# Cross-attention queries with features on partitions, and their rms in the exponential's scale

## The chip, the core and the metric

The kernel runs on one core of a Trainium2 chip. The time is device time in microseconds of one execution; the figure to compare is the median of several runs. Engines are named as in the profile: PE is TensorE (matrix products and transposes; PEld its weight loads), DVE is VectorE, ACT is ScalarE, POOL is GpSimd, SP is SyncE, which issues most DMAs.

## What is computed

One layer of a streaming encoder, on 1024 tokens of width 1024 in float32: a mixer (forgetting attention and gated linear attention side by side) with an output projection, cross-attention on 256 memory tokens, and an MLP, each added to the residual `h`. The part that matters here:

```python
def memory_cross_attention(hn, memn, wq, wkv, q_norm_g, k_norm_g, wo):
    B, S, _ = hn.shape                       # 1, 1024
    M = memn.shape[1]                        # 256
    q = rms_norm((hn @ wq).reshape(B, S, XATTN_HEADS, XATTN_HEAD_DIM), q_norm_g)   # 4 heads of 256
    k, v = jnp.split(memn @ wkv, 2, axis=-1)
    k = rms_norm(k.reshape(B, M, XATTN_HEADS, XATTN_HEAD_DIM), k_norm_g)
    v = v.reshape(B, M, XATTN_HEADS, XATTN_HEAD_DIM)
    s = jnp.einsum('bshd,bmhd->bhsm', q, k).astype(jnp.float32) / math.sqrt(XATTN_HEAD_DIM)
    p = jax.nn.softmax(s, axis=-1)
    o = jnp.einsum('bhsm,bmhd->bshd', p.astype(v.dtype), v).reshape(B, S, D_MODEL)
    return o @ wo

h = h + memory_cross_attention(rms_norm(h, norm_xattn_g), rms_norm(mem, norm_mem_g), ...)
```

`rms_norm` divides by the root of the mean square over the last axis, plus an epsilon.

## The kernel before

**Products.** Every float32 operand is split into a high part and a remainder (`sh`/`sl`, `wh`/`wl`, `qh`/`ql`, `th`/`tl`, `oh`/`ol`): ACT writes the high part, DVE the remainder. A product is then three matrix products, high x high, high x remainder, remainder x high (`gemm`, lines L110 to L112). `evac_split` (L117, L118) does such a split out of PSUM.

**Layout.** `self.h` holds the residual with features on partitions: `h[:, k, t]`, eight blocks `k` of 128 features by 1024 tokens. The gain of the norm ahead of the queries is in the weights (`wsplit` with `C_XAT`, L99/L100); the norm's own factor per token goes into the rms of the heads as an epsilon scaled by the token's mean square (`hev`).

**Order of the stages.** `project_out` (L838) makes `h`, in two halves of 512 tokens; for each of eight feature blocks it loads a partial result (`hr`, L851), adds it (L856), squares the block (L169) and adds the square on POOL to `acc` (L170). Four transposes of `acc` per half (`token_squares`, L177) and small operations (L179, L180, L860, L861) then make the tokens' mean squares `hv` and `hev`. Next come `xattn` (L958), `project_o_first` (L879), `project_o_rest` (L887) and the MLP. The instructions are written in this order; the framework's scheduler then reorders each engine's queue by its own estimate of a timeline, places the pools, and sets semaphores, so neighbouring stages overlap, and early MLP weights (`raw` of `in_mlp_w`, split into `g` by L1075/L1076) are loaded and split during cross-attention where room is free.

**Cross-attention.** Two groups `n` of two heads, four units `u` of 256 tokens each, eight units in all. `queries(n, u)` takes 128 tokens at a time: `split_tile` (L819/L820) splits `h` into a 128x1024 pair, 24 products of 512 columns put tokens on partitions (`mm`), ACT squares them (L144), DVE sums per head (L146), POOL makes the rms (L129/L130), DVE scales (`qn`, L995), PE transposes four 128x128 blocks (L998), and `evac_split` writes `qh`, `ql`. `attend(n, u)` comes one unit later: scores of 256 columns per head (`s`), the maximum (L1014), exponentials (L1020), reciprocal (L1021), normalising on POOL (L1024), transposes (L1027), the split `th`/`tl`, the values `pv` in products of 256 columns, and the split `o`, which SP writes to memory (`od`, L1038). `load_o` (L868/L869) reads `od` back for the output projection, whose products carry `mm<-oh,wh`; the first four blocks of that are in `project_o_first`.

Of the kernel before, what the change touches and what calls it, by code (L numbers as in the profile page):

```python
# [51 lines left out]
class Layer:  # L52
# [757 lines left out]

    def split_tile(self, sp, srcs, kt=KT):

        nc = self.nc
        sh = self.T(sp, [P, kt, P], F32R, "sh")
        sl = self.T(sp, [P, kt, P], F32R, "sl")
        k = 0
        for src in srcs:
            w = src.shape[1]
            nc.scalar.activation(sh[:, k:k + w, :], src, AF.Copy)  # L819
            nc.vector.tensor_tensor(sl[:, k:k + w, :], src, f(sh[:, k:k + w, :]), ALU.subtract)  # L820
            k += w
        return [sh[:, k, :] for k in range(kt)], [sl[:, k, :] for k in range(kt)]

# [54 lines left out]

    def project_o_first(self):  # L879

        self.ost, self.O = ExitStack(), {}
        self.load_o(self.open(self.ost, "op0", side="right"), 1)
        self.Wo = self.wsplit(self.wo[:, 0:512], None)
        for i in range(4):
            self.o_block(self.Wo, 0, 1, i, self.T(self.mmp, [P, 512], F32, "mm"))
# [72 lines left out]
    def xattn(self):  # L958
        nc = self.nc
        with ExitStack() as st:  # L960
            kvp = [None, self.open(st, "kv41")]
            qp = self.open(st, "q4", 3)
            qnp = self.open(st, "qn4", 2)
            pp = self.open(st, "p4", 3)
            ptp = self.open(st, "pt4", 2)
            mmp, trp = self.mmp, self.trp
            kst = ExitStack()
            kvp[0] = self.open(kst, "kv40")
            sst = ExitStack()
            sp = self.open(sst, "sp", 2, side="right")  # L970
# [4 lines left out]
            Ws, KV = {}, {}  # L975

            def weights(n):
                Ws[n] = self.wsplit(self.wq[:, n * 512:(n + 1) * 512], C_XAT)
                kT = self.T(kvp[n], [P, 2, 4, M], F32R, "kT")
                nc.sync.dma_start(f(kT), self.kTd[:, :, 4 * n:4 * n + 4, :])  # L980
                vm = self.T(kvp[n], [P, 2, 2, 512], F32R, "vm")
                nc.sync.dma_start(f(vm), self.vmd[:, :, :, n * 512:(n + 1) * 512])
                KV[n] = kT, vm

            def queries(n, u):
                qh = self.T(qp, [P, 2, 4, P], F32R, "qh")
                ql = self.T(qp, [P, 2, 4, P], F32R, "ql")
                for i in range(2):
                    t = 2 * u + i
                    A = self.split_tile(sp, (self.h[:, :, t * P:(t + 1) * P],))  # L990
                    ps = self.T(mmp, [P, 512], F32, "mm")
                    self.gemm(ps, *A, *Ws[n])
                    qn = self.T(qnp, [P, 512], F32, "qn")
                    r = self.head_rstd(ps, qn, 2, self.hev[:, t:t + 1])
                    nc.vector.tensor_tensor(v2(qn), v2(ps), self.bcast(r, 256), ALU.mult)  # L995
                    tp = self.T(trp, [P, 512], F32, "tr")
                    for j in range(4):
                        nc.tensor.transpose(tp[:, j * P:(j + 1) * P], qn[:, j * P:(j + 1) * P], self.ident)  # L998
                    self.evac_split(qh[:, i], ql[:, i], v4(tp))
                return qh, ql  # L1000

            def attend(n, u, q):
                qh, ql = q
                kT, vm = KV[n]
                th = self.T(ptp, [P, 2, 4, P], F32R, "th")
                tl = self.T(ptp, [P, 2, 4, P], F32R, "tl")
                for i in range(2):
                    ps = self.T(sps, [P, 512], F32, "s")
                    for h in range(2):
                        ks = (2 * h, 2 * h + 1)  # L1010
                        self.gemm(ps[:, h * M:(h + 1) * M], [qh[:, i, k, :] for k in ks], [ql[:, i, k, :] for k in ks],
                                  [kT[:, 0, k, :] for k in ks], [kT[:, 1, k, :] for k in ks])
                    nm = self.T(self.smallp, [P, 2], F32, "nm2")
                    nc.vector.tensor_reduce(nm, v2(ps), AX.X, ALU.max, negate=True)  # L1014
                    p = self.T(pp, [P, 512], F32, "p")
                    rs = self.T(self.smallp, [P, 2], F32, "rs2")
                    rr = self.T(self.smallp, [P, 2], F32, "rr2")
                    for h in range(2):
                        c = slice(h * M, (h + 1) * M)
                        nc.scalar.activation(p[:, c], ps[:, c], AF.Exp, bias=nm[:, h:h + 1], accum_out=rs[:, h:h + 1])  # L1020
                    nc.vector.reciprocal(rr, rs)  # L1021
                    for h in range(2):
                        c = slice(h * M, (h + 1) * M)
                        nc.gpsimd.tensor_scalar(p[:, c], p[:, c], rr[:, h:h + 1], 1.0, ALU.mult, ALU.mult)  # L1024
                    tp = self.T(trp, [P, 512], F32, "tr")
                    for j in range(4):
                        nc.tensor.transpose(tp[:, j * P:(j + 1) * P], p[:, j * P:(j + 1) * P], self.ident)  # L1027
                    self.evac_split(th[:, i], tl[:, i], v4(tp))
                for h in range(2):
                    pv = self.T(pvp, [P, 2, 2, P], F32, "pv")  # L1030
                    for d in range(2):
                        c = slice((2 * h + d) * P, (2 * h + d + 1) * P)
                        self.gemm(pv[:, d], [vm[:, 0, m, c] for m in range(2)], [vm[:, 1, m, c] for m in range(2)],
                                  [th[:, :, 2 * h + m, :] for m in range(2)], [tl[:, :, 2 * h + m, :] for m in range(2)])
                    o = self.T(pp, [P, 2, 2, 256], F32R, "o")
                    self.evac_split(o[:, 0], o[:, 1], pv.rearrange("p d t s -> p d (t s)"))
                    for i in range(2):
                        nc.sync.dma_start(self.od[:, i, u // 2, 4 * n + 2 * h:4 * n + 2 * h + 2,  # L1038
                                                  u % 2 * 256:u % 2 * 256 + 256], f(o[:, i]))

            units = [(0, u) for u in range(4)] + [(1, u) for u in (2, 3, 0, 1)]
            q = []
            for i, (n, u) in enumerate(units):
                if i % 4 == 0:
                    weights(n)
                q.append(queries(n, u))
                if i >= 1:
                    attend(*units[i - 1], q[i - 1])
                if i == 4:
                    kst.close()  # L1050
            sst.close()
            attend(*units[-1], q[-1])
            self.project_o_first()

# [286 lines left out]
```

## Time and profile before

| | |
|---|---|
| median of 3 runs | 1450.64 us (1450.14 to 1451.19) |
| the profiled execution | 1454.34 us |
| its span, first to last instruction | 1452.6 us |
| mean granted clock of PE | 0.996 |
| PE busy | 1427.7 us, 98% of the span |
| DVE, ACT, POOL busy | 65%, 47%, 27% |
| cross-attention, about | 592 to 755 us of the span |

How the rows below are read. In a timeline row stand the start in us, the length in us, engine, line, operation, out<-in by the program's names, shapes, how many were put together (x2), and in brackets the idle time before it on its engine and what ended that. Matrix products overlap, so the time from start to start counts, not the length. A windows row has the stretch, its length, the busy time and count of PE, PEld, DVE, ACT, POOL, then the granted clock of PE (1.00 is full), the share of the DMA engines and GB/s. A waits row has the waiting engine, tile and line, what ended the wait, and then total us, number, and longest. A groups row has line, engine, operation, tiles, shapes and count, then busy us and the mean of one in ns, then idle time ahead of them. Rows of two numbers and an engine are pieces of the chain of work that ended last.

### The profile page before, as it was taken

The page shows a single profiled execution, that of the slowest core. Times are in us where ns is not written, and L with a number is a line of the kernel's source. Part 1 is how long each engine was busy: PE and PEld are TensorE (multiplying, and loading weights), DVE is VectorE, ACT ScalarE, POOL GpSimd, SP SyncE. Part 2 cuts the span into 40 slices and gives each one's busy share as a digit, 9 for nine tenths or more (in the row PEclk, how much of TensorE's full clock was granted, in tenths as well). Part 3 has the DMA queues.
Part 4 walks back from the last instruction along what each step waited for, and adds up shares of the span by engine and source line. Part 5 has one row for each costly group of instructions (what it writes and reads, how often), then busy time and mean ns, then how long its engine had stood idle before and what let it go on. Part 6 is the DMA issues. An engine that isn't in the chain of part 4 may idle for free.

```text
span 1452.6 us, 19224 instructions
## 1 busy us (share of the span) xinstructions
PE 1427.7 (98%) x7068; PEld 1190.0 (82%) x7068; DVE 948.6 (65%) x1354; ACT 679.9 (47%) x1095; POOL 397.1 (27%) x404
## 2 busy tenths in 40 slices
PE   9999999998999999999999999999999999999998
PEld 7788788887888887888888878887888888888887
DVE  5366732428798776666644895636556968788796
ACT  4444341327678565455542364445546735335230
POOL 3235513312242223521212300000000542333454
PEclk9999999999999999999999999999999999999999
DMA  8435520268677642412474124444445835336353
GB/s 273 128 73 131 138 70 1 73 176 252 203 211 234 188 140 87 132 59 88 150 266 170 51 80 153 174 174 189 174 174 209 322 121 188 131 122 225 119 198 119
DMA packets 121166, 223.94 MB, mean 154 GB/s; under 512 B 8912, under 2 KB 54512, under 8 KB 118512
## 3 DMA queue, kind: packets, MB, share of 16 engines
q1 hardware_dynamic: 119776, 218.25, 46.5%
q10 hardware_dynamic: 1296, 4.46, 1.0%
q8 instruction: 56, 0.92, 0.3%
q14 instruction: 38, 0.31, 0.1%
HBM read 150.59 MB, written 72.09 MB: 153 GB/s over the span
## 4 chain that ended last, share of the span: by engine, by line
PE 71%; issue 16%; DMA 6%; DVE 3%; ACT 2%; POOL 1%; ACTq 0%; SPq 0%; DVEq 0%; POOLq 0%
PE mm L110 13%; PE mm L112 13%; PE mm L111 13%; PE my L111 5%; PE my L112 5%; PE my L110 5%; PE tr L111 2%; PE tr L112 2%; PE tr L110 2%; PE tr L696 2%; PE pv L703 1%; DMA xt<-in_x_dram 1%; DMA raw<-in_w_in_dram 1%; PE pv L704 1%; PE s L656 1%
## 5 line engine op out<-in xcount | busy, mean ns | idle before, releaser
L111 PE MATMUL my<-x,g 128*128 128x512 f32 x464 | 180.6, 389 | 1.3 <-DVE x L1076 1.3
L110 PE MATMUL my<-x,g 128*128 128x512 f32 x464 | 180.6, 390 | 0.4 <-ACT h L1281 0.4
L112 PE MATMUL my<-x,g 128*128 128x512 f32 x464 | 180.5, 389 | 0.0
L111 PE MATMUL mm<-wl,xh 128*128 128x512 f32 x320 | 126.5, 396 | 0.9 <-DVE wl L100 0.8
L110 PE MATMUL mm<-wh,xh 128*128 128x512 f32 x320 | 126.0, 397 | 1.0 <-DVE sq L307 1.0
L112 PE MATMUL mm<-wh,xl 128*128 128x512 f32 x320 | 125.9, 394 | 0.0
L1075 ACT ACTIVATE g<-s 128x1024 fp32r<-128x1024 f32 (+1 forms) x72 | 68.7, 962 | 105.0 <-PE my L112 39.1
L1076 DVE TENSOR_TENSOR g<-raw,g 128x512 fp32r<-128x512 f32 (+3 forms) x72 | 69.2, 964 | 67.6 <-ACT g L1075 67.4
L111 PEld LDWEIGHTS my<-x,g 128*128 128x128 f32 x464 | 87.1, 188 | 19.9 <-DVE x L1076 1.7
L1101 POOL TENSOR_TENSOR s<-raw 128x384 f32<-128x384 f32 (+1 forms) x20 | 25.8, 1291 | 282.7 <-DVE h L1196 213.8
L110 PEld LDWEIGHTS my<-x,g 128*128 128x128 f32 x464 | 87.1, 188 | 18.8 <-ACT h L1281 0.8
L1075 ACT ACTIVATE g<-raw 128x512 fp32r<-128x512 f32 (+3 forms) x72 | 55.5, 773 | 100.3 <-DMA raw<-in_mlp_w_dram 40.1
L112 PEld LDWEIGHTS my<-x,g 128*128 128x128 f32 x464 | 87.1, 188 | 17.9
L667 POOL TENSOR_SCALAR p<-p,rrec 128x128 f32<-128x128 f32 (+3 forms) x64 | 57.9, 907 | 159.2 <-DVE rrec L666 151.9
L1076 DVE TENSOR_TENSOR g<-s,g 128x1024 fp32r<-128x1024 f32 (+1 forms) x72 | 88.2, 1228 | 7.6 <-ACT g L1075 7.5
L1243 DVE TENSOR_TENSOR x<-x 128x1024 fp32r<-128x1024 f32 (+1 forms) x64 | 76.8, 1220 | 17.3 <-ACT x L1242 17.1
L110 PE MATMUL mm<-x,g 128*128 128x512 f32 x220 | 85.8, 390 | 0.0
L112 PE MATMUL mm<-x,g 128*128 128x512 f32 x220 | 85.7, 389 | 0.0
L111 PE MATMUL mm<-x,g 128*128 128x512 f32 x220 | 85.6, 389 | 0.0
L110 PE MATMUL tr<-x,g 128*128 128x512 f32 x212 | 82.5, 389 | 0.0
L111 PE MATMUL tr<-x,g 128*128 128x512 f32 x212 | 82.5, 389 | 0.0
L112 PE MATMUL tr<-x,g 128*128 128x512 f32 x212 | 82.5, 389 | 0.0
(318 smaller groups left out, 3739.2 us busy)
## 6 DMA issues: line engine op xcount, KB each, us to landing
ud<-h SPq DMA_DIRECT2D x32, 768.0 KB, 3.8
x<-ud SPq DMA_DIRECT2D x48, 512.0 KB, 5.3
raw<-in_mlp_w_dram SPq DMA_DIRECT2D x20, 1024.0 KB, 7.4
raw<-in_mlp_w_dram SPq DMA_DIRECT2D x16, 768.0 KB, 6.0
raw<-in_w_in_dram SPq DMA_DIRECT2D x23, 512.0 KB, 5.0
raw<-in_xattn_wkv_dram SPq DMA_DIRECT2D x16, 512.0 KB, 7.4
od<-o SPq DMA_DIRECT2D x32, 256.0 KB, 4.0
ud<-h SPq DMA_DIRECT2D x32, 256.0 KB, 2.8
```

Source lines behind the costliest of these rows:

```text
L110: mm(ps, lh[k], rh[k], start=start and k == 0, stop=False, **kw)
L111: mm(ps, lh[k], rl[k], start=False, stop=False, **kw)
L112: mm(ps, ll[k], rh[k], start=False, stop=stop and k == n - 1, **kw)
L656: nc.tensor.matmul(ps[:, c], qa[:, ts], ka[:, c], start=True, stop=False)
L667: nc.gpsimd.tensor_scalar(p[:, 0:n], p[:, 0:n], rr, 1.0, ALU.mult, ALU.mult)
L696: nc.tensor.transpose(o, pp[i][:, kb * P:(kb + 1) * P], self.ident)
L703: nc.tensor.matmul(pv, va[:, kb, :], th[:, js], start=kb == 0, stop=False)
L704: nc.tensor.matmul(pv, va[:, kb, :], tl[:, js], start=False, stop=kb == nb - 1)
L1075: self.nc.scalar.activation(hi, src, AF.Copy)
L1076: self.nc.vector.tensor_tensor(lo, src, f(hi), ALU.subtract)
L1101: eng.tensor_tensor(s[:, 0], raw[:, 3], raw[:, 2], ALU.add)
L1243: nc.vector.tensor_tensor(lo, f(lo), f(hi), ALU.subtract)
```

## The change

The queries are made with features on partitions, for 512 tokens at a time. The weights are the stationary side, the split `h` the moving side. So nothing is transposed to get `q`. Its rms is not applied to `q`: the squares of a head's two feature blocks are added on POOL, transposed (four 128x128 blocks for two blocks of features), summed on DVE, and POOL makes `rq`, which is the `scale=` of the exponential and multiplies the maximum. There are four units of 512 tokens, in the order (n, half) = (0, 0), (0, 1), (1, 1), (1, 0). The values become products of 512 columns, and `od` is written by 16 DMAs of 512 KB instead of 32 of 256 KB. The pool of split `h` holds 12 pairs of 512 columns (48 KB a partition, 16 KB before), keys and values have one buffer, which is loaded again at the third unit, and the last unit's scores and values stand between the loads and blocks of the output projection. `split_tile` and `project_o_first` are gone. In the changed kernel lines behind 810 move: the h addition is L842, the loads of `oh`/`ol` L854/L855, squares L981, their addition L985, their transposes L988, exponentials L1018, POOL's normalising L1022, transposes of p L1025, `od` L1039, the MLP's splits L1096/L1097.

```diff
+            def query(u, W, A, j):
+                ps = self.T(mmp, [P, 512], F32, "mm")
+                c = slice(j * P, (j + 1) * P)
+                self.gemm(ps, *([w[:, c] for w in w_] for w_ in W), *zip(*A))
+                q = self.T(qp, [P, 2, 512], F32R, "q")
+                self.evac_split(q[:, 0], q[:, 1], ps)
+                Q.setdefault(u, []).append(q)
+                sq = self.T(sqp, [P, 512], F32, "sq")
+                nc.scalar.activation(sq, ps, AF.Square)
+                if j % 2 == 0:
+                    self.sq0 = sq
+                    return
+                nc.gpsimd.tensor_tensor(sq, sq, self.sq0, ALU.add)
+                tp = self.T(trp, [P, 512], F32, "tr")
+                for t in range(4):
+                    nc.tensor.transpose(tp[:, t * P:(t + 1) * P], sq[:, t * P:(t + 1) * P], self.ident)
+                ss = self.T(self.smallp, [P, 4], F32, "ss4")
+                nc.vector.tensor_reduce(ss, v4(tp), AX.X, ALU.add)
+                nc.gpsimd.tensor_scalar(ss, ss, 1.0 / 256, None, ALU.mult)
+                half = units[u][1]
+                nc.gpsimd.tensor_tensor(ss, ss, self.hev[:, 4 * half:4 * half + 4], ALU.add)
+                if j == 1:
+                    R[u] = self.T(self.smallp, [P, 2, 4], F32, "rq")
+                nc.gpsimd.tensor_tensor(R[u][:, j // 2, :], ss, self.mhalf[:, 0:4], ALU.pow)
...
+            def scores(u, t):
...
+                r = R[u][:, :, t]
+                nc.vector.tensor_reduce(nm, v2(ps), AX.X, ALU.max, negate=True)
+                nc.vector.tensor_tensor(nm, nm, r, ALU.mult)
...
-                        nc.scalar.activation(p[:, c], ps[:, c], AF.Exp, bias=nm[:, h:h + 1], accum_out=rs[:, h:h + 1])
+                    nc.scalar.activation(p[:, c], ps[:, c], AF.Exp, bias=nm[:, h:h + 1], scale=r[:, h:h + 1], accum_out=rs[:, h:h + 1])
...
+            def values(u):
...
+                for j in range(4):
+                    pv = self.T(pvp, [P, 512], F32, "pv")
+                    c, ms = slice(j * P, (j + 1) * P), (2 * (j // 2), 2 * (j // 2) + 1)
+                    self.gemm(pv, *([vm[:, i, m, c] for m in range(2)] for i in range(2)),
+                              [th[:, m] for m in ms], [tl[:, m] for m in ms])
...
+                    nc.sync.dma_start(self.od[:, :, half, 4 * n + j, :], f(o))
...
-            sp = self.open(sst, "sp", 2, side="right")
+            sp = self.open(sst, "sp", 12, side="right")
...
+            for u, (n, half) in enumerate(units):
+                if u % 2 == 0:
+                    W = self.wsplit(self.wq[:, n * 512:(n + 1) * 512], C_XAT)
+                if u == 0:
+                    memory(0)
+                    A = split(half, range(KT))
+                keep = A
+                for j in range(4):
+                    if j == 3 and u in (0, 2):
+                        A = split(units[u + 1][1], range(4))
+                    query(u, W, keep, j)
+                    if u and j < 2:
+                        scores(u - 1, 2 * j)
+                        scores(u - 1, 2 * j + 1)
+                    elif u and j == 2:
+                        values(u - 1)
+                        if u == 2:
+                            memory(1)
+                if u in (0, 2):
+                    A = A + split(units[u + 1][1], range(4, KT))
             sst.close()
-            attend(*units[-1], q[-1])
-            self.project_o_first()
+            self.ost, self.O = ExitStack(), {}
+            self.load_o(self.open(self.ost, "op0", side="right"), 1)
+            self.Wo = self.wsplit(self.wo[:, 0:512], None)
+            for t in range(4):
+                scores(3, t)
+            for i in range(4):
+                if i == 2:
+                    values(3)
+                self.o_block(self.Wo, 0, 1, i, self.T(self.mmp, [P, 512], F32, "mm"))
```

Three places where the order of an engine changes. Numbers behind names tell buffers apart; brackets name the semaphores that an instruction waits for, by the engine or DMA queue that raises them.

First, ACT at the end of project_out, where the first splits of `h` for the queries stand. Before, two 128x1024 splits (`sh_6226`, `sh_6271`) stand among the squares of the second half, without a wait:

```order
L169 ACTIVATE sqT_5970<-h_5805 128x512 [waits DVE_49,Pool_49]
L169 ACTIVATE sqT_5983<-h_5805 128x512 [waits DVE_49,Pool_49]
L819 ACTIVATE sh_6226<-h_5805 128x1024
L819 ACTIVATE sh_6271<-h_5805 128x1024
L166 ACTIVATE acc_1376_5813<-h_5805 128x512 [waits DVE_49]
L169 ACTIVATE sqT_6045<-h_5805 128x512 [waits DVE_49,Pool_49]
```

After, the first split of 512 columns stands behind the last square:

```order
L99 ACTIVATE wh_6743<-raw_6741,cols_74 128x512 [waits DMAHW2_49,PE_49]
L169 ACTIVATE sqT_6122<-h_5805 128x512 [waits DVE_49,Pool_49]
L169 ACTIVATE sqT_6135<-h_5805 128x512 [waits DVE_49,Pool_49]
L117 ACTIVATE sh_6221<-h_5805 128x512 [waits DMAHW4_49,DMAHW5_49,DMAHW3_49,DMAHW6_49,DMAHW0_49,DMAHW7_49,PE_49,Pool_49]
L117 ACTIVATE sh_6225<-h_5805 128x512
L117 ACTIVATE sh_6229<-h_5805 128x512
```

What moved: the first split now waits for loads of `hr`, for PE's last transpose of `acc` (`tr_6138`) and for POOL's last addition (of `sqT_6135`); the larger pool lies on the room of project_out's `acc`, `sqT` and `hr`.

Second, PE there. Before, the transposes of `acc` stand between query products, 39 products behind the last of project_out:

```order
L110 MATMUL mm_6275<-wh_6202,sh_6271 128x512
L111 MATMUL mm_6275<-wl_6203,sh_6271 128x512
L112 MATMUL mm_6275<-wh_6202,sl_6272 128x512
L177 MATMUL tr_6138<-ident_75,acc_1376_5813 128x128 [waits Pool_49]
L177 MATMUL tr_6138<-ident_75,acc_1376_5813 128x128 x3
L110 MATMUL mm_6275<-wh_6206,sh_6271 128x512
L111 MATMUL mm_6275<-wl_6207,sh_6271 128x512
```

After, they stand between project_out's last product (`mm_6127`) and the first query product (`mm_6253`):

```order
L111 MATMUL mm_6127<-sl_6009,wh_5840 128x512
L112 MATMUL mm_6127<-sh_6008,wl_5841 128x512
L177 MATMUL tr_6138<-ident_75,acc_1376_5813 128x128 [waits Pool_49]
L177 MATMUL tr_6138<-ident_75,acc_1376_5813 128x128 x3
L110 MATMUL mm_6253<-sh_6221,wh_6179 128x512 [waits DMAHW3_49,DMAHW4_49,DMAHW2_49,DMAHW5_49,DMAHW1_49,DMAHW6_49,DMAHW0_49,DMAHW7_49,DVE_49,Activation_49]
L110 MATMUL mm_6283<-sh_6221,wh_6179 128x512
L111 MATMUL mm_6253<-sl_6222,wh_6179 128x512 [waits DVE_49]
```

What moved: the transposes that wait for POOL are now ahead of all query products.

Third, ACT behind the last query product. Before, the last unit's exponentials (`p`) stand among evacuations alone:

```order
L1020 ACTIVATE p_7709,rs_1777_7710<-s_7694,nm_1775_7707 128x256 [waits DVE_49,Pool_49]
L117 ACTIVATE th_7593<-tr_7648 128x512 [waits PE_49]
L117 ACTIVATE th_7692<-tr_7717 128x512 [waits PE_49,Activation_49]
L1020 ACTIVATE p_7739,rs_1783_7740<-s_7724,nm_1781_7737 128x256 [waits DVE_49,Pool_49]
L117 ACTIVATE o_7668<-pv_7655 128x512 [waits DMAHW7_49,DMAHW1_49,PE_49]
```

After, two splits of MLP weights (`g`) stand ahead of the third of four tiles' exponentials (`p_7577`):

```order
L1018 ACTIVATE p_7546,rs_1753_7547<-s_7530,nm_1751_7543,rq_7264 128x256 [waits DVE_49]
L1096 ACTIVATE g_1846_8203<-raw_1845_8201 128x512 [waits DMAHW3_49]
L1096 ACTIVATE g_1848_8208<-raw_1847_8206 128x512 [waits DMAHW4_49]
L117 ACTIVATE th_7497<-tr_7523 128x4x128 [waits PE_49,Activation_49]
L1018 ACTIVATE p_7577,rs_1759_7578<-s_7561,nm_1757_7574,rq_7264 128x256 [waits DVE_49]
L117 ACTIVATE th_7497<-tr_7554 128x4x128 [waits PE_49]
L117 ACTIVATE o_7398<-pv_7391 128x512 [waits DMAHW6_49,Activation_49]
```

What moved: exponentials of the last tiles are queued behind loads of MLP weights, which SP issues behind the first loads of `oh` and `ol`.

More of the change, by code (lines that the diff above doesn't have):

```diff
@@ L808, in out_part @@
                 yield
[L811 to L822, printed above, removed]
     def split_half(self, sp, src, half, bufs, ks):
@@ L1002, in attend @@
[L1002 to L1028, printed above, removed]
-                for h in range(2):
[L1030 to L1050, printed above, removed]
-            sst.close()
-            attend(*units[-1], q[-1])
-            self.project_o_first()
+            def split(half, ks):
+                out = []
+                for k in ks:
+                    sh = self.T(sp, [P, 512], F32R, "sh")
+                    sl = self.T(sp, [P, 512], F32R, "sl")
+                    self.evac_split(sh, sl, self.h[:, k, half * 512:(half + 1) * 512])
+                    out.append((sh, sl))
+                return out
@@ new lines, in scores @@
+            def scores(u, t):
+                kT = KV[units[u][0]][0]
+                ts = slice(t * P, (t + 1) * P)
+                if t == 0:
+                    TH[u] = [self.T(ptp, [P, 4, 512], F32R, n) for n in ("th", "tl")]
+                ps = self.T(sps, [P, 512], F32, "s")
+                for h in range(2):
+                    ks = (2 * h, 2 * h + 1)
+                    self.gemm(ps[:, h * M:(h + 1) * M], *([Q[u][k][:, i, ts] for k in ks] for i in range(2)),
+                              *([kT[:, i, k, :] for k in ks] for i in range(2)))
+                r = R[u][:, :, t]
+                nm = self.T(self.smallp, [P, 2], F32, "nm2")
+                nc.vector.tensor_reduce(nm, v2(ps), AX.X, ALU.max, negate=True)
+                nc.vector.tensor_tensor(nm, nm, r, ALU.mult)
+                p = self.T(pp, [P, 512], F32, "p")
+                rs = self.T(self.smallp, [P, 2], F32, "rs2")
+                rr = self.T(self.smallp, [P, 2], F32, "rr2")
+                for h in range(2):
+                    c = slice(h * M, (h + 1) * M)
+                    nc.scalar.activation(p[:, c], ps[:, c], AF.Exp, bias=nm[:, h:h + 1], scale=r[:, h:h + 1], accum_out=rs[:, h:h + 1])
+                nc.vector.reciprocal(rr, rs)
+                for h in range(2):
+                    c = slice(h * M, (h + 1) * M)
+                    nc.gpsimd.tensor_scalar(p[:, c], p[:, c], rr[:, h:h + 1], 1.0, ALU.mult, ALU.mult)
+                tp = self.T(trp, [P, 512], F32, "tr")
+                for j in range(4):
+                    nc.tensor.transpose(tp[:, j * P:(j + 1) * P], p[:, j * P:(j + 1) * P], self.ident)
+                self.evac_split(*(v[:, :, ts] for v in TH[u]), v4(tp))
@@ new lines, in xattn @@
+            units = [(0, 0), (0, 1), (1, 1), (1, 0)]
+            A = []
+            for u, (n, half) in enumerate(units):
[5 more added lines that the diff above has]
+                keep = A
+                for j in range(4):
+                    if j == 3 and u in (0, 2):
[10 more added lines that the diff above has]
+                    A = A + split(units[u + 1][1], range(4, KT))
```

46 lines of the change are left out of this document (13 added, 33 removed).

## The prediction

> **What bounds the kernel now.** I read the page's busy shares first, then a window over the whole cross-attention stage, then the waits of PE in that stage.
>
> ```profile
> span 1452.6 us, 19224 instructions
> PE 1427.7 (98%) x7068; PEld 1190.0 (82%) x7068; DVE 948.6 (65%) x1354; ACT 679.9 (47%) x1095; POOL 397.1 (27%) x404
> 592.00:754.00 162.00, 160.74 (x955) 141.39 (x954) 97.56 (x156) 79.18 (x165) 40.31 (x72) 1.00 0.41 135
> PE mm L110 <- DMA oh<-od: 0.8, 1, 0.8
> PE mm L111 <- DMA ol<-od: 0.4, 2, 0.2
> ```
>
> PE works through 160.74 of 162 us at full clock, and its three waits (1.27 us) are all for loads of the attention output at the end. So only PE work removed is a gain, and each new PE wait is a loss. The profiled execution took 1454.34 us, span 1452.6; the median is 1450.64. I sum differences and add them to both.
>
> **PE work removed.** Rows of PE at the start of the stage, one row pair of the values, the group of query transposes, and two pieces of the chain of work:
>
> ```profile
> 591.94 0.39 PE L112 MATMUL mm<-sh,wl 128*128 128x512 f32 x1
> 592.16 0.39 PE L110 MATMUL mm<-wh,sh 128*128 128x512 f32 x1
> 592.39 0.39 PE L111 MATMUL mm<-wl,sh 128*128 128x512 f32 x1
> 742.72 0.28 PE L110 MATMUL pv<-th,vm 128*128 128x256 f32 x1
> 742.84 0.28 PE L111 MATMUL pv<-tl,vm 128*128 128x256 f32 x1
> L998 PE MATMUL tr<-ident,qn 128*128 128x128 f32 x64 | 10.1, 272 | 0.0
> 601.17 0.44 PE tr L177 x4
> 611.17 0.44 PE tr L998 x4
> ```
>
> Starts of neighbours give the pitch: 0.227 us for 512 columns, 0.12 for 256. The 384 query products keep 512 columns, and the 192 score products 256: nothing. The values become 96 products of 512 instead of 192 of 256: 96 x 0.227 = 21.8 against 192 x 0.12 = 23.0, so -1.25. The 64 transposes of `qn` (16 groups of four, 0.44 each on the chain) become 32 of summed squares: 8 x 0.44 = -3.5. Sum -4.75, certain within half a microsecond.
>
> The Trainium skill, page "TensorE: Matmul & The Clock Gate", section "Back-to-back issue gap", gives about 131 ns for a sustained product of 512 columns; the values' 96 products would then be an estimated 12.6 us, a gain of 10.4 instead of 1.25. This trace shows 227 ns for such products, and the sum goes by that row.
>
> ACT and DVE lose scaling and `qn` splits and gain products with r; both have over 60 us idle in the stage. Their sums cost nothing while PE has queued matmuls. The new chain square, POOL addition, transpose, reduce, POOL power ends in `scale=` of an exponential one unit later, with a whole unit's query products (96 x 0.227 = 21.8 us) as cover: 0. The keys and values reloaded at unit 2 into a single buffer have the same cover: 0, at worst the 0.83 that one late load costs PE below.
>
> **The start.** Before, ACT splits the first two token tiles while project_out still runs, so the query product at 592.16 follows the last product of project_out directly; the transposes of the accumulated squares (L177) come 9 us later, between query products. After, `sh_6221` waits for these very transposes and for POOL's last addition, and PE has nothing ahead of its consumer.
>
> ```profile
> 578.46 1.99 ACT L819 ACTIVATE sh<-h 128x1024 fp32r<-128x1024 f32 x2
> 579.60 3.71 DVE L820 TENSOR_TENSOR sl<-h,sh 128x1024 fp32r<-128x1024 f32 x2 [0.63 <-ACT sh L819]
> 586.60 3.35 SPq L80 DMA_DIRECT2D raw<-in_xattn_wq_dram  x2
> 590.17 0.94 SPq L851 DMA_DIRECT2D hr<-hpd  x2
> 594.90 1.34 DVE L856 TENSOR_TENSOR h<-mm,hr 128x512 f32<-128x512 f32 x2 [2.10 <-DMA hr<-hpd]
> 595.68 1.28 ACT L169 ACTIVATE sqT<-h 128x512 f32<-128x512 f32 x2 [0.72 <-DVE h L856]
> 591.69 4.41 POOL L170 TENSOR_TENSOR acc<-acc,sqT 128x512 f32<-128x512 f32 x3 [0.67 <-ACT sqT L169]
> 596.46 3.30 POOL L170 TENSOR_TENSOR acc<-acc,sqT 128x512 f32<-128x512 f32 x2 [0.36 <-ACT sqT L169]
> 601.01 0.60 PE L177 MATMUL tr<-ident,acc 128*128 128x128 f32 x4
> 604.93 0.59 ACT L117 ACTIVATE qh<-tr 128x512 fp32r<-128x512 f32 x1
> 606.31 0.68 DVE L118 TENSOR_TENSOR ql<-tr,qh 128x512 fp32r<-128x512 f32 x1
> ```
>
> POOL's last addition ends at 599.76. Ahead of it stand, in turn, the load of the last two residuals (issued 590.17, used 594.90), the two h additions on DVE, the two squares on ACT and two additions of 1.65 on POOL. That is the upper end. DVE is freed of the 3.71 us of `sl`, which stood ahead of the h addition that releases this load, so all of it may come earlier. The lower end: project_out's last five blocks end, counted back from 592.2 by 6 products of 0.227 each, at 590.8, 589.4, 588.1 and 586.7; behind the first of the five come h 0.69, square 0.63 and then five additions (4.41 + 3.30): 595.8. I take 599.1, near the upper end, because the wait before 594.90 was ended by the load and not by DVE, and two query weight loads still go out ahead of it on SP. Then the transposes 0.60 and the first split 0.60: first product at 600.3 instead of 592.16, less 0.44 for the transposes that no longer come in between, plus 0.2 because the first remainder (0.68) has only two products to cover it: +7.9, between 4.6 and 8.6. From there one split (0.6 on ACT, 0.7 on DVE) feeds six products (1.36), so PE stays fed.
>
> **The clock.** Windows around two places where PE idled before, and the products in the first:
>
> ```profile
> 335.00:339.00 4.00, 2.70 (x6) 2.15 (x7) 4.00 (x7) 2.78 (x7) 2.48 (x2) 0.55 1.05 390
> 339.00:343.00 4.00, 4.00 (x18) 3.22 (x16) 4.00 (x10) 2.72 (x6) 1.86 (x1) 0.60 1.05 356
> 535.00:539.00 4.00, 3.30 (x14) 2.72 (x15) 3.82 (x10) 3.60 (x10) 0.45 (x2) 0.72 0.62 194
> 539.00:543.00 4.00, 3.55 (x25) 3.04 (x24) 3.01 (x7) 2.46 (x7) 1.28 (x3) 0.85 0.00 1
> 336.30 0.79 PE L112 MATMUL mm<-sh,wl 128*128 128x512 f32 x1 [1.53 <-DVE wl L93]
> 336.89 0.63 PE L110 MATMUL mm<-sh,wh 128*128 128x512 f32 x1
> 337.31 0.63 PE L111 MATMUL mm<-sl,wh 128*128 128x512 f32 x1
> ```
>
> The granted clock fell to half after idle of about 3 us in all: two windows missing (0.45 + 0.40) x 4 = 3.4 us, and (0.28 + 0.15) x 4 = 1.7. The pitch there is 0.42. A single idle of 8 us is longer, so I expect one spell and take 2.5, between the two rows; its ends are 0 (no spell) and 3.4. The Trainium skill, same page, section "What's actually happening", has half rate after an idle window of some 3.4 us and full rate again after a busy one; that would be an estimated 1.7 here, and both spells of this trace fit it roughly.
>
> **The end.** Rows of SP, PE, ACT, POOL and DVE behind the last query product, at whose end SP issues the first output load (723.61), a window, and one line of the DMA issues:
>
> ```profile
> 723.61 0.34 SPq L868 DMA_DIRECT2D oh<-od  x1
> 730.48 0.50 PE L111 MATMUL mm<-ol,wh 128*128 128x512 f32 x1 [0.24 <-DMA ol<-od]
> 741.69 0.73 PE L110 MATMUL mm<-oh,wh 128*128 128x512 f32 x2 [0.83 <-DMA oh<-od]
> 724.00:742.00 18.00, 16.74 (x114) 14.89 (x113) 11.54 (x21) 9.83 (x26) 3.78 (x8) 1.00 0.92 310
> 736.94 0.47 ACT L1020 ACTIVATE p<-s,nm 128x256 f32<-128x256 f32 x1
> 737.75 0.20 ACT L1020 ACTIVATION_READ_ACCUMULATOR p<-s,nm 128x1 f32 x1
> 738.25 0.94 POOL L1024 TENSOR_SCALAR p<-p,rr 128x256 f32<-128x256 f32 x2 [4.32 <-DVE rr L1021]
> 740.90 0.69 DVE L1014 TENSOR_REDUCE nm<-s 128x2 f32<-128x512 f32 x1 [0.30 <-PE s L112]
> raw<-in_mlp_w_dram SPq DMA_DIRECT2D x20, 1024.0 KB, 7.4
> ```
>
> Call the end of the last query product E. Both kernels issue the output loads at E, and the first remainder `ol` landed 6.9 us later. After, PE has 24 score products (2.9) and 12 value products (2.7) ahead of them: 5.6, so it waits between 0.4 and 1.3; I take 0.9. Before, almost two units of attention stood there.
>
> From there PE finds work until about E + 18.7: 24 output products (5.4), 12 value products (2.7), the last squares' transposes (0.44), the third and fourth tiles' scores (2.9) and the first two tiles' transposes (0.9). Then it wants the third tile's probabilities. Its scores end at E + 16.4. Two 1 MB loads of MLP weights, their splits on ACT and their remainders on DVE stand ahead of that tile's exponentials now; before, the two such splits of this stage stood between queries. So two remainders and the maximum follow on DVE (3 x 0.69: E + 18.5), the product with r (two numbers a partition; 0.1 allowed), two exponentials with their sums (1.0, from 736.94 to 737.95: E + 19.7), a reciprocal behind two other steps of DVE (E + 20.15) and the first half on POOL (0.47): E + 20.6, a wait of 1.9. The fourth tile's exponentials follow two evacuations and those of the third: another 1.9. Its `th` and `tl` take 0.8 more than the two output products cover, and the output load behind the writes of `o`, which wait on SP behind the MLP loads, 0.5. Sum 0.9 + 1.9 + 1.9 + 0.8 + 0.5 = 6.0 against 1.27 before: +4.7.
>
> That is with the MLP weights landed in time. They are issued at E + 2.9; 7.4 behind that is E + 10. If the 5.5 MB that are issued from E on, or still under way, go in order at 310 GB/s, the second lands at E + 18: 1.3 more on the third tile, and 2 on the last output load, +8. The other end is +0, where only loads make PE wait, as before.
>
> **Sum.** -4.75 + 7.9 + 2.5 + 4.7 = +10.35: 1461.0 for the median, 1464.7 for a profiled execution like this.
>
> **Rivals.**
> 1. Only the gap at the start comes: the clock stays up and the chains at the end are hidden. -4.75 + 7.9 = +3.2, 1453.8. For it: at 738.25 such a chain passed without a PE wait. Against: two units' products covered it there, and the idle is longer than those that cost the clock before.
> 2. The end is worse: the MLP weights land late (+8), or a second half-clock spell follows the waits there (+2.5). With one, 1463.5 to 1464.3; with both, 1466.8. For it: DMA was at 0.92 of its share from 724 to 742, and idle of 3 us in pieces was enough at 336. Against: the median landing of 7.4.
> 3. Not slower: POOL's last addition comes as early as 595.8, because freeing DVE moves the whole chain. The gap is 4.6, the clock stays and the end is hidden: -0.15, 1450.5. It decides from an end before 596 on; above that the gap is more than the 4.75 saved. Against: the load that ended the wait.
> 4. The change's gain without its wait: `sh_6221` finds its wait met when project_out ends. -4.75, 1445.9. Against: PE's own order puts the L177 transposes ahead of every query product, and POOL was 7.4 us behind PE there.
> 5. Wide products cost no more than narrow ones: the values at 96 x 0.12 = 11.5 save 10.3 more, and the main case becomes 1450.7. Against: all 384 query products at 0.227. The 131 ns of the section "Back-to-back issue gap" (the Trainium skill, "TensorE: Matmul & The Clock Gate") speaks for it.
>
> **Chances.** Main 0.50 (1456 to 1463.5), rival 1 0.20, rival 2 0.18, rival 3 0.07, rival 4 0.04, rival 5 0.01. A measurement tells about 0.2%, 2.9 us, from no change. A quarter of rival 1, most of rival 3 and rival 5 fall within it: same 0.12. Faster 0.05 (rival 4 and the early edge of rival 3), slower 0.83. The range 1453.0 to 1467.0 leaves out rivals 3 to 5, the lower edge of rival 1 and what lies beyond rival 2.
>
> **What would show it.** After: an idle of PE of 6 to 8.5 us at the stage's start, released by ACT's split (L117) or the L177 transposes; granted clock below 1 for some us behind it; 96 value rows with pitch 0.227; PE waits before L1025 transposes, released by POOL, of 2 to 4 us in all. I am wrong if POOL's last L170 addition ends before 596, if the clock stays 1.00, or if ACT's g rows do not hold the exponentials.

## The result, and the profile after

The changed kernel took 1475.03 us (median of four runs; 1471.99 to 1475.34 without the profiled one), the kernel before 1450.91 in the same call: a ratio of 1.0150, interval 1.0124 to 1.0176, without the profiled one. By that ratio it is slower by some 22 us; the forecast was +10.35, and its range ended at 1467.

The execution profiled with that result ran at a mean granted clock of 0.555 (2390.71 us) and is left out. The profile shown here is of the same kernel in a second run, `a0_after`: 1471.14 us (1469.97 to 1475.04) against 1453.05, ratio 1.0115, interval 1.0089 to 1.0141. The profiled execution took 1475.04 us, 20.7 more than that of before.

The page's busy shares, which answer to those of before:

```profile
span 1473.2 us, 18909 instructions
PE 1439.0 (98%) x6940; PEld 1182.1 (80%) x6940; DVE 936.9 (64%) x1354; ACT 681.1 (46%) x1103; POOL 399.8 (27%) x404
```

PE issues 128 instructions fewer, as the change says (96 values, 32 transposes), yet is busy 11.3 us longer. So about half of the loss is not idle time (the busy time at half clock is in it). The waits of PE in cross-attention, 10.4 us against 1.27 before, hold the other half:

```profile
PE tr L177 <- POOL acc L170: 6.3, 1, 6.3
PE tr L1025 <- POOL p L1022: 2.7, 2, 1.6
PE mm L110 <- ACT sh L117: 0.8, 1, 0.8
PE mm L111 <- DMA ol<-od: 0.6, 1, 0.6
```

The start of the stage on PE, in order of time, with some rows between 600.83 and 603.82 left out, then two rows of the values, then POOL ahead of the transposes:

```profile
590.84 0.39 PE L112 MATMUL mm<-sh,wl 128*128 128x512 f32 x1
597.50 1.12 PE L177 MATMUL tr<-ident,acc 128*128 128x128 f32 x4 [6.27 <-POOL acc L170]
599.38 1.22 PE L110 MATMUL mm<-sh,wh 128*128 128x512 f32 x2 [0.77 <-ACT sh L117]
600.40 0.63 PE L111 MATMUL mm<-sl,wh 128*128 128x512 f32 x1
600.83 0.63 PE L112 MATMUL mm<-sh,wl 128*128 128x512 f32 x1
603.82 0.48 PE L110 MATMUL mm<-sh,wh 128*128 128x512 f32 x1
604.13 0.40 PE L111 MATMUL mm<-sl,wh 128*128 128x512 f32 x1
604.37 0.40 PE L112 MATMUL mm<-sh,wl 128*128 128x512 f32 x1
660.20 0.39 PE L111 MATMUL pv<-tl,vm 128*128 128x512 f32 x1
660.43 0.40 PE L112 MATMUL pv<-th,vm 128*128 128x512 f32 x1
```

```profile
594.23 3.22 POOL L170 TENSOR_TENSOR acc<-acc,sqT 128x512 f32<-128x512 f32 x2 [0.17 <-ACT sqT L169]
```

The gap, the wait for POOL's additions and then for ACT's first split, and ten products in 4.44 us until 603.82 (most of them 0.427 apart) are all there. POOL's last addition (the row by itself) ends at 597.45, 6.4 us behind project_out's last product. The last two rows are values of 512 columns: 0.23. Windows, first around the start, then at the end of the stage, then in the rest of the output projection and the MLP, which the change does not touch:

```profile
590.00:600.00 10.00, 2.96 (x12) 1.91 (x10) 5.80 (x9) 4.85 (x9) 7.61 (x6) 0.69 0.39 129
600.00:610.00 10.00, 10.00 (x37) 7.96 (x36) 6.68 (x12) 5.06 (x10) 2.01 (x3) 0.80 0.01 2
750.00:760.00 10.00, 9.98 (x43) 8.29 (x44) 3.57 (x9) 1.80 (x3) 0.39 (x1) 0.83 0.82 300
800.00:1400.00 600.00, 597.07 (x2601) 485.92 (x2600) 420.46 (x492) 279.25 (x337) 109.89 (x80) 1.00 0.44 159
```

The same last window of the kernel before:

```profile
800.00:1400.00 600.00, 597.09 (x2641) 493.69 (x2640) 429.42 (x506) 286.08 (x346) 115.59 (x82) 1.00 0.47 168
```

This is the reading that the forecast lacked. At full clock, with PE busy for 597.1 of 600 us in both, the changed kernel gets through 40 matmuls fewer: 40 x 0.227 = 9.1 us. Neighbours in the MLP show it, first of before, then of after:

```profile
1249.87 0.39 PE L110 MATMUL mm<-x,g 128*128 128x512 f32 x1
1250.10 0.39 PE L111 MATMUL mm<-x,g 128*128 128x512 f32 x1
1250.32 0.39 PE L112 MATMUL mm<-x,g 128*128 128x512 f32 x1
1250.55 0.39 PE L110 MATMUL mm<-x,g 128*128 128x512 f32 x1
```

```profile
1289.93 0.39 PE L110 MATMUL mm<-x,g 128*128 128x512 f32 x1
1290.16 0.40 PE L111 MATMUL mm<-x,g 128*128 128x512 f32 x1
1290.40 0.39 PE L112 MATMUL mm<-x,g 128*128 128x512 f32 x1
1290.63 0.40 PE L110 MATMUL mm<-x,g 128*128 128x512 f32 x1
```

Lengths are alike (0.39 to 0.40), starts are not: 0.68 us over three steps before, 0.70 after, so 0.227 and 0.233 apart, for products of the same shape and the same tiles.

### The profile page after: what moved, and what is told of

It reads as the page before. It is cut to its first block, busy times and chain, and to the rows that moved or that the text cites. A ratio compares the mean times of both kernels' runs of the same rounds, so it can differ in the third digit from the quotient of the medians.

```text
span 2388.9 us, 18909 instructions
## 1 busy us (share of the span) xinstructions
PE 2371.6 (99%) x6940; PEld 1434.6 (60%) x6940; DVE 934.1 (39%) x1354; ACT 692.5 (29%) x1103; POOL 375.1 (16%) x404
## 4 chain that ended last, share of the span: by engine, by line
PE 98%; DMA 1%; DVE 0%; POOL 0%; issue 0%; ACT 0%; SPq 0%; DVEq 0%; POOLq 0%; ACTq 0%
PE mm L110 17%; PE mm L112 17%; PE mm L111 17%; PE my L111 7%; PE my L110 7%; PE my L112 7%; PE tr L111 4%; PE tr L112 4%; PE tr L110 4%; PE tr L696 2%; PE pv L704 1%; PE pv L703 1%; PE s L656 1%; PE s L657 1%; PE go L551 1%; PE ga L545 1%
## 5 line engine op out<-in xcount | busy, mean ns | idle before, releaser
L111 PE MATMUL my<-x,g 128*128 128x512 f32 x464 | 268.0, 578 | 0.0
L112 PE MATMUL my<-x,g 128*128 128x512 f32 x464 | 267.4, 577 | 0.0
L110 PE MATMUL my<-x,g 128*128 128x512 f32 x464 | 267.1, 576 | 0.0
L111 PE MATMUL mm<-wl,xh 128*128 128x512 f32 x320 | 186.2, 582 | 0.0
L112 PE MATMUL mm<-wh,xl 128*128 128x512 f32 x320 | 185.9, 581 | 0.0
L110 PE MATMUL mm<-wh,xh 128*128 128x512 f32 x320 | 185.2, 583 | 0.0
L112 PE MATMUL mm<-sh,wl 128*128 128x512 f32 x256 | 149.2, 584 | 1.4 <-DVE wl L93 1.4
L110 PE MATMUL mm<-sh,wh 128*128 128x512 f32 x256 | 149.5, 586 | 0.8 <-ACT sh L117 0.8
L1096 ACT ACTIVATE g<-s 128x1024 fp32r<-128x1024 f32 (+1 forms) x72 | 69.0, 962 | 277.0 <-PE my L112 119.3
L111 PEld LDWEIGHTS my<-x,g 128*128 128x128 f32 x464 | 101.6, 219 | 77.1 <-issue 45.9
L111 PE MATMUL mm<-sl,wh 128*128 128x512 f32 x256 | 147.7, 578 | 0.0
L112 PEld LDWEIGHTS my<-x,g 128*128 128x128 f32 x464 | 101.3, 218 | 76.3 <-issue 44.1
L110 PEld LDWEIGHTS my<-x,g 128*128 128x128 f32 x464 | 100.9, 218 | 76.9 <-issue 44.9
L1097 DVE TENSOR_TENSOR g<-raw,g 128x512 fp32r<-128x512 f32 (+3 forms) x72 | 64.9, 903 | 166.3 <-ACT g L1096 166.2
L111 PE MATMUL mm<-x,g 128*128 128x512 f32 x220 | 127.1, 578 | 0.0
L110 PE MATMUL mm<-x,g 128*128 128x512 f32 x220 | 127.0, 577 | 0.0
L112 PE MATMUL mm<-x,g 128*128 128x512 f32 x220 | 126.3, 574 | 0.0
L112 PE MATMUL tr<-x,g 128*128 128x512 f32 x212 | 122.3, 577 | 0.0
L111 PE MATMUL tr<-x,g 128*128 128x512 f32 x212 | 122.1, 576 | 0.0
L110 PE MATMUL tr<-x,g 128*128 128x512 f32 x212 | 122.0, 575 | 0.0
L1096 ACT ACTIVATE g<-raw 128x512 fp32r<-128x512 f32 (+3 forms) x72 | 55.4, 773 | 191.5 <-PE my L112 78.3
```

Source lines behind the costliest of these rows:

```text
L110: mm(ps, lh[k], rh[k], start=start and k == 0, stop=False, **kw)
L111: mm(ps, lh[k], rl[k], start=False, stop=False, **kw)
L112: mm(ps, ll[k], rh[k], start=False, stop=stop and k == n - 1, **kw)
L1096: self.nc.scalar.activation(hi, src, AF.Copy)
L1097: self.nc.vector.tensor_tensor(lo, src, f(hi), ALU.subtract)
```

## The experiments

### Why untouched products are slower: where the tiles lie

Outside the stage that was changed, the addresses in the built kernels differ in one respect. The new small tile `rq`, six buffers in the pool of small tiles, takes six slots of 32 bytes a partition, 192 bytes. All pools that are placed behind it from the same end move up by 192; those placed from the other end stay. In the kernel before, the moving and the stationary tile of each of the 5316 products of 512 columns begin 224 bytes above a multiple of 256. After, 1956 of 5412 pair a tile at 160 with one at 224. Theory A: the pitch is longer where the two sides differ. Its rival: something in the new stage (load on DMA, DVE or ACT, or another order) slows the MLP.

**`e2_rq8`**, the changed kernel with 256 bytes instead of 192, in the same order on every engine:

```diff
-                    R[u] = self.T(self.smallp, [P, 2, 4], F32, "rq")
+                    R[u] = self.T(self.smallp, [P, 2, 4], F32, "rq", bufs=8)
```

> The changed kernel with 8 buffers for rq instead of 6 (64 bytes a partition more); nothing left out, the same order on every engine. Theory D (addresses): products of 512 columns start every 0.2267 us when the moving and the stationary tile lie at equal places modulo 128 bytes, and up to 0.2333 when not; rq's 192 bytes shifted the tiles on the left side against those on the right, and this costs 12 to 15 us, mostly in the MLP, which the change doesn't touch. With 256 bytes the sides agree again: 1456 to 1460, pitch 0.2267 throughout the MLP, start gap and end as in the changed kernel. Theory E (the slower pitch comes with the changed instructions or a lower clock of that stretch, not with addresses): no change, 1470 to 1475.

**`e3_rq4`**, the same with `bufs=4`, a shift of 128 bytes:

> The changed kernel with 4 buffers for rq instead of 6: a shift of 128 bytes, so the two sides agree modulo 128 but not modulo 256. Theory D with modulus 128: as with 8 buffers, 1456 to 1460. Theory D with modulus 256 or more: as the changed kernel, 1470 to 1475, pitch near 0.231 in the MLP. Theory E: 1470 to 1475.

**`b1_pad192`**, the kernel before with an unused tile of the same 192 bytes:

```diff
+        self.T(self.smallp, [P, 8], F32, "pad")
```

> The kernel before with six unused small tiles of 32 bytes in the pool of small tiles: 192 bytes a partition, nothing computed with them. Theory D: the MLP's pitch rises to about 0.231 and the time by 11 to 15 us, 1461 to 1466, with no other new wait of PE. Theory E: no change, 1450 to 1453.

**`b3_both`**, `b1_pad192` with 64 bytes more ahead of the pools at the other end, so that all tiles have moved and both sides stand at 160:

```diff
+            self.T(self.open(st, "padr", side="right"), [P, 16], F32, "padr")
```

> The kernel before with two unused pads: the 192 bytes of the small tiles as in the run with one pad, and 64 bytes ahead of the pools that are placed from the other end. All tiles stand elsewhere than before, yet every moving and every stationary tile of a 512-column product lies at 160 above a multiple of 256 bytes, so both sides again agree. Relative place (the cost comes where moving and stationary tile differ modulo 256): pitch 0.227 everywhere, 1450 to 1454, same. Absolute place (224 is good, 160 is bad, or a pool moved off its line of 256 costs by itself): pitch 0.230 to 0.233, 1463 to 1468. A cost of the pad's own instructions can be ruled out in both: it is never written.

The window of 800 to 1400 us, of `e2_rq8`, `e3_rq4`, `b1_pad192` and `b3_both` in this order:

```profile
800.00:1400.00 600.00, 595.88 (x2637) 492.68 (x2636) 424.20 (x500) 283.16 (x341) 113.81 (x82) 1.00 0.45 162
```

```profile
800.00:1400.00 600.00, 597.45 (x2608) 487.47 (x2607) 421.80 (x493) 279.82 (x338) 110.67 (x80) 1.00 0.44 159
```

```profile
800.00:1400.00 600.00, 597.51 (x2602) 486.44 (x2601) 422.95 (x495) 281.82 (x339) 108.72 (x79) 1.00 0.45 161
```

```profile
800.00:1400.00 600.00, 597.45 (x2643) 494.55 (x2642) 431.25 (x506) 285.42 (x344) 118.60 (x84) 1.00 0.47 168
```

| | moving, stationary tile modulo 256 | median us | ratio to before, interval |
|---|---|---|---|
| `e2_rq8` | all 224, 224 | 1464.26 | 1.0072 (1.0046 to 1.0097) |
| `e3_rq4` | 96 and 224, mixed | 1475.13 | 1.0151 (1.0128 to 1.0174) |
| `b1_pad192` | 160 and 224, mixed | 1465.78 | 1.0091 (1.0062 to 1.0119) |
| `b3_both` | all 160, 160 | 1452.83 | 0.9995 (0.9982 to 1.0008) |

The last row of the table settles it against the rival. An unused tile of 192 bytes costs the kernel before 13 us (9 to 17), and 64 more unused bytes at the other end give them all back. So it is neither the change's own work nor a given address: what counts is how the two sides lie to each other. A shift of 128 bytes costs as much as one of 192. With `rq` in four buffers the changed kernel takes 11 us more than with eight (1475.13 less 1464.26, same call; some 5 either way); with six, measured in two other calls, the ratios 1.0150 and 1.0115 against 1.0072 make 6 to 11. `e2_rq8` stayed above the 1456 to 1460 that its expectation gave, since the 12 to 15 deducted there were too much.

Means from start to start between neighbours of one kind, in the window of 800 to 1400 us. The starts are the trace's, the addresses those of the built kernels; steps over 300 ns are left out. A row is a number of products of one kind that follow each other on PE:

| run | moving, stationary modulo 256 | products in the row | steps | mean ns |
|---|---|---|---|---|
| `before` | 224, 224 | over 24 | 2572 | 226.7 |
| `b3_both` | 160, 160 | over 24 | 2576 | 226.7 |
| `a0_after` | 160, 160 | over 24 | 679 | 227.1 |
| `a0_after` | 160, 160 | up to 12 | 117 | 231.5 |
| `a0_after` | 160, 224 | any | 857 | 233.3 |
| `a0_after` | 224, 160 | any | 228 | 231.4 |
| `a0_after` | 224, 224 | 13 to 24, the longest there | 244 | 228.3 |
| `a0_after` | 224, 224 | up to 12 | 158 | 230.6 |

The mixed ones are slow. Like pairs are back at 227 in long rows, but not in short rows between mixed ones. Why a neighbour of another kind counts stays open. Added up over all steps from one product of 512 columns to the next behind 605 us, outside the spells of half clock, what is over 226.7 ns makes 13.2 us in `a0_after`, 10.4 of it on mixed pairs, and 0.9 us in the kernel before: 12.3 us more.

### The start

**`e1_rooms`** leaves the addresses as they are and takes away what makes the first split wait. One pool of 12 pairs must wait for all that it is laid over; of three pools of 4 the first need not.

```diff
-            sp = self.open(sst, "sp", 12, side="right")
+            spa, spb, spc = (self.open(sst, n, 4, side="right") for n in ("spa", "spb", "spc"))
+            rooms = iter([spa, spb, spc, spa, spb, spc])
...
-                for k in ks:
+                for i, k in enumerate(ks):
+                    if i % 4 == 0:
+                        sp = next(rooms)
```

> The changed kernel with its pool of split h made of three pools of four pairs instead of one of twelve, so that the first four feature blocks get the room that was free before, and only the others wait for project_out. Nothing is left out. In the order the transposes of acc (L177) now stand behind 39 query products. Theory A: the start gap and its half clock go, 8 to 15 us less than the changed kernel: 1459 to 1467. Theory B: only the gap itself goes, 7 to 9 us: 1466 to 1468, and the waits at the end stay. Theory C: as B. If the first splits are not what holds PE: no change, 1472 to 1476.

It took 1464.24 us, ratio 1.0068 (1.0046 to 1.0091), 6.9 less than `a0_after` in the same call: a little less than either theory's saving. PE at the start of the stage, and a window over it:

```profile
589.82 0.39 PE L112 MATMUL mm<-sh,wl 128*128 128x512 f32 x1
590.60 0.51 PE L110 MATMUL mm<-sh,wh 128*128 128x512 f32 x1 [0.39 <-DVE h L842]
590.94 0.40 PE L111 MATMUL mm<-sl,wh 128*128 128x512 f32 x1
599.65 0.60 PE L177 MATMUL tr<-ident,acc 128*128 128x128 f32 x4
580.00:600.00 20.00, 19.61 (x90) 1.00 0.50 157
```

The query products follow project_out with 0.39 of idle, and the transposes of the squares come 9 us later, between products, as before the change. This window has PE alone: busy 19.61 of 20 us, at a granted clock of 1.00, so the half clock is gone too, as theory A of this expectation has it.

**`e4_rooms_rq8`** has both repairs, the rooms and the like addresses.

> Three pools for the split h and 8 buffers for rq together. Theory D: the gap at the start and the slower pitch are both gone, what is left is 4.75 of work saved against the waits at the end: 1448 to 1453. Theory E: as the three pools alone, 1462 to 1465.

It took 1452.21 us in 10 runs, ratio 1.0002 (0.9988 to 1.0016). Against `e2_rq8` of the same call the rooms took away 12.0 us. So the start with its half clock is worth 7 to 12 us (7.9 and 2.2 by the steps below), and both repairs together bring the changed kernel level with the one before. That leaves the saved 4.75 to be found. The waits at the end of the stage, a window with a spell of half clock behind them, and what ACT, POOL and DVE do ahead of them, in `e4_rooms_rq8` (exponentials are L1021 here, POOL's normalising L1025, transposes of p L1028, MLP splits L1099):

```profile
PE tr L1028 <- POOL p L1025: 2.9, 2, 2.3
PE s L110 <- ACT p L1021: 1.7, 1, 1.7
740.00:750.00 10.00, 9.67 (x41) 8.06 (x42) 3.73 (x8) 2.21 (x4) 0.71 (x2) 0.83 0.69 241
```

```profile
726.32 1.16 ACT L88 ACTIVATE wh<-raw 128x512 fp32r<-128x512 f32 x2 [4.19 <-DMA raw<-in_xattn_wo_dram]
726.98 1.29 DVE L93 TENSOR_TENSOR wl<-raw,wh 128x512 fp32r<-128x512 f32 x2 [2.47 <-ACT wh L88]
728.20 0.68 DVE L993 TENSOR_REDUCE ss<-tr 128x4 f32<-128x512 f32 x1
729.57 1.50 POOL L999 TENSOR_TENSOR rq<-ss,mhalf 128x4 f32<-128x4 f32 x1
731.30 0.56 ACT L1021 ACTIVATE p<-s,nm,rq 128x256 f32<-128x256 f32 x1 [1.36 <-DVE nm L1015]
733.48 0.63 ACT L1099 ACTIVATE g<-raw 128x512 fp32r<-128x512 f32 x1
735.91 0.60 ACT L117 ACTIVATE th<-tr 128x512 fp32r<-128x512 f32 x1 [0.79 <-PE tr L1028]
```

A late load of output weights holds ACT, ACT holds `wl` on DVE, `wl` stands ahead of the sum of the last squares, and only behind that come `rq` (until 731.07) and the first exponential. An MLP split (733.48) then stands between the exponentials and the next splits, but ACT idles 0.79 us before `th`, so it is not what holds that.

### The end

**`e5_raw_late`** is `e4_rooms_rq8` with the pool of raw MLP weights opened two lines later, behind those of the first `g` tiles. The two loads of 1 MB and their splits then come after the stage.

```diff
-            self.raw7 = self.open(mx, "raw7", 2, side="right", **kw)
...
+            self.raw7 = self.open(mx, "raw7", 2, side="right", **kw)
```

> As the kernel with three pools and 8 buffers for rq, and in the output projection the pool of raw MLP weights is opened behind the two pools of split weights, so that its room is one that cross-attention's end still uses: the two 1 MB loads and their splits leave the end of the stage. Nothing is left out. The kernel without this last edit has PE waits of 4.6 us at the end of the stage and 3.4 us of half clock. Theory F (the MLP weights crowd DMA and stand ahead of the rms and the exponentials on ACT and DVE): waits fall to 2.5 us or less, the half clock goes, 3 to 4 us less: 1447.5 to 1449.5, faster than the kernel before by 3 to 5. Theory G (the chain of maximum, exponentials, reciprocal, POOL and transposes of the last tiles is itself longer than what covers it): 4 us or more of waits before the transposes of p remain, 1450 to 1453. Rival H: the MLP, whose weights come later, waits at its start: 1453 or more, with PE waits behind 800.

It took 1448.10 us, ratio 0.9972 (0.9961 to 0.9983): 4.1 us faster than the kernel before (2.5 to 5.7). Its waits in the stage:

```profile
PE mm L110 <- DMA oh<-od: 1.6, 1, 1.6
PE s L110 <- ACT p L1021: 1.0, 1, 1.0
PE mm L111 <- DMA ol<-od: 0.8, 1, 0.8
PE mm L110 <- DVE h L842: 0.4, 1, 0.4
```

The wait for POOL's probabilities (2.9) is gone. Most of what is left is for output loads, as before the change; at the end 3.4 us are left, more than the 2.5 that theory F allowed. The edit took away the loads and the splits together, so which of the two held the chain is not parted.

**`b2_raw_late`** makes the same edit in the kernel before.

> The kernel before with the pool of the raw MLP weights opened behind those of the first g tiles, so that no 1 MB load and no g split stands in the end of cross-attention: the same edit that took 4.1 us off the changed kernel with room and aligned small tiles. Theory (that edit only pays where attention ends in waits of its own): before waits 1.27 us there, all for output loads, so -1.3 to 0, and if the late loads make the MLP's first products wait, up to +2; 1449 to 1453, same. Rival (the edit pays by itself, since late MLP loads spare PE something elsewhere): -4, 1447 to 1449, and then the changed layout of the queries has gained nothing.

1453.94 us against 1453.09, ratio 0.9998 (0.9985 to 1.0012): nothing. So moving those loads paid only in the kernel whose attention ends the stage with its own chain, and the 4.1 us belong to the changed kernel.

**`e6_wo_first`** is `e5_raw_late` with the output weights' loads ahead of the second half of the output loads:

```diff
-            self.load_o(self.open(self.ost, "op0", side="right"), 1)
...
+            self.load_o(self.open(self.ost, "op0", side="right"), 1)
```

> The changed kernel with room for split h, rq in eight buffers and the late MLP loads, and besides the output weights' loads issued ahead of the loads of the second half of the attention output. Theory: 3.5 us of waits were left at the end, 1.0 for the exponentials and 2.4 for loads of the output; the remainder of the output weights that held DVE comes earlier, so the wait for exponentials goes (-1), while the output loads behind 2 MB of weights land later (+1 to +3): 1447 to 1451, within 0.2% of the kernel without this edit. Rival (the loads were late because of the MLP weights alone): output loads land as before and 1446 to 1447.5.

1450.30 us, ratio 0.9983 (0.9971 to 0.9995). The interval overlaps that of `e5_raw_late`, so which is better can't be told. Its waits:

```profile
PE mm L110 <- DMA oh<-od: 1.7, 1, 1.7
PE mm L111 <- DMA ol<-od: 0.8, 1, 0.8
PE s L110 <- ACT p L1021: 0.2, 1, 0.2
```

The wait for exponentials fell from 1.0 to 0.2, as the theory had it; the waits for output loads grew neither longer (the theory) nor shorter.

## Why the prediction was right or wrong

By its steps, from the profile after:

| step | predicted | measured | from |
|---|---|---|---|
| PE work removed | -4.75 | not seen by itself | see below |
| the start | +7.9 | +7.9 | 591.07 to 599.38, less 0.44 |
| the clock | +2.5 | +2.2 | ten products in 4.44 us instead of 2.27 |
| the end | +4.7 | +3.8 | waits 0.6 + 1.6 + 1.1, half clock 1.7, less 1.27 |
| untouched products | 0 | +11.6 | what is left of 20.7; 12.3 added up from the starts; `b1_pad192`: 13 |

**The step that failed** is the one on PE work removed: "The 384 query products keep 512 columns ... nothing". It took 0.227 as the price of a shape, and all products outside the stage as unchanged without a word. The price also hangs on where both tiles lie, and `rq`, of which the forecast counted only the instructions that make it, moved one of the two sides of 1956 products. The trace of before couldn't have shown this: there all products are of one kind. The addresses of the two kernels could have shown that they moved, though not the price. In place of nothing the runs show 11.6 to 13 us: steps of 227 ns grew to 231 to 233, the 192 unused bytes of `b1_pad192` alone bring the loss, and `b3_both` takes it away again.

`e2_rq8` is the change with like addresses, and its +10.5 us (6.7 to 14.1) is where the forecast of +10.35 stood. So the other four terms hold together as a sum; with the three measured sizes it makes +9.2. That it comes so close is in part luck, given the width of the interval.

**PE work removed** could only be checked by differences. `e4_rooms_rq8` has 4.6 of waits at the end and about 1.7 lost to a half clock there, less 1.27: +5.0, and it measured level with before (+0.3, some 2 either way), so about 4.7 was saved. `e6_wo_first` has 3.0 of waits in all, less 1.27, which makes -3.0; measured were -2.5 (-4.2 to -0.7). `e5_raw_late` has 3.4 at the end and 0.4 at the start, less 1.27: +2.5, which makes -2.2; measured were -4.1 (-5.7 to -2.5), so it gained nearly 2 us more than this account has, and why is open. Values of 512 columns went at 0.23 as said, and rival 5 fell: the 131 ns that the Trainium skill gives (page "TensorE: Matmul & The Clock Gate", section "Back-to-back issue gap") appear in no run here, where the mean is 226.7 at the least.

**The start** was right in cause, and in size with some luck: the first product came 8.3 us behind project_out's last, as against 8.1 forecast, and POOL's additions were the last link: 6.4 us behind project_out, taken as 6.9. That half microsecond was lost again on the transposes, which took 1.12 at half clock instead of 0.60. Rival 3 falls with it (its point was 3.8, 596), and rival 4, which came true only in `e1_rooms`, where it was made so.

**The clock** came near, though the 2.5 was chosen between two rows and not worked out from a length. Windows 0.69 and 0.80 lack 5.1 us of clock, a spell of 10.2 us, of which some 4.7 fell on idle time. The Trainium skill, page "TensorE: Matmul & The Clock Gate", section "What's actually happening", has half rate after an idle window of some 3.4 us; the spell here is as long as three such windows, so the 1.7 estimated from one was short (2.2 on the ten products and 0.5 on the transposes).

**The end** was right in the waits that it named and near in size, but the part of the `g` splits in it isn't shown. The third tile's wait was 1.64 where 1.9 was forecast, the fourth's 1.07 for 1.9, the first output load's 0.62 for 0.9. The terms 0.8 and 0.5 did not come, but a half clock of 3.4 us (window 0.83, 1.7 lost) did, which the forecast had put into rival 2. Rows of `a0_after`:

```profile
742.68 1.39 ACT L1096 ACTIVATE g<-raw 128x512 fp32r<-128x512 f32 x2
745.32 0.60 ACT L117 ACTIVATE th<-tr 128x512 fp32r<-128x512 f32 x1 [1.26 <-PE tr L1025]
745.81 0.56 ACT L1018 ACTIVATE p<-s,nm,rq 128x256 f32<-128x256 f32 x1
748.02 0.89 PE L1025 MATMUL tr<-ident,p 128*128 128x128 f32 x4 [1.64 <-POOL p L1022]
```

The two `g` splits stand ahead of the third tile's exponential, as said, and start without a wait, so the late landing of rival 2 did not come. But ACT then idles 1.26 us until PE has transposed, and `th` stands ahead of the exponential too, so on ACT the splits did not hold it. With loads and splits gone in `e5_raw_late`, the wait for POOL is gone; by which of the two is open. Rival 1 fell with the clock and the end. That the last squares' sum waits behind `wl` in `e4_rooms_rq8` was not foreseen; in `a0_after` it waits for PE's transposes.

## What to carry to other kernels

Where a kernel's PE is busy 98% of the time, compare PE's instruction count in an untouched window of equal length before explaining any wait: 2601 against 2641 showed half of this loss at once. Here a new small tile of 192 bytes a partition moved every pool behind it; compare the start of moving and stationary tiles modulo 256 bytes with the kernel before, and pad to keep them alike. And a pool that grows can move the start of a stage behind the end of the one before: three pools of 4 instead of one of 12 took away 7 to 12 us with the same work.

## What the hardware showed that was not expected

A product of 512 columns starts 227 ns after its neighbour where the moving and the stationary tile lie alike modulo 256 bytes, whether at 224 (`e2_rq8`, 2637 matmuls in 600 us) or at 160 (`b3_both`, 2643), and 231 to 233 ns where they lie 64 bytes apart. Short rows of like pairs between mixed ones are slow too (231 to 232). Over the whole window a matmul of the mixed kernels takes 0.230 to 0.231 us on average. Shifts of 128 (2608) and 192 bytes (2602) cost about the same. What in the chip does this was not tried, nor were shifts under 64 bytes.
